# RWKV-7 chain in a hybrid decoder step: two heads per 128 by 128 product, states on diagonal blocks

## The chip, the cores and the metric

The kernel runs on one core of one Trainium2 chip. The metric is the time of one execution on the device in microseconds (us). Three runs of the kernel before took 1861.98, 1864.36 and 1865.9 us; the median, 1864.36 us, is what the change is measured against. One more execution was profiled; its own time stands in the profile section.

## What is computed

One decoder layer for 1024 prompt tokens and 64 sample tokens (8 sequences of 8). A combined projection feeds a sliding-window attention branch and an RWKV-7 branch; both are gated, projected, merged and projected again. The change touches the RWKV-7 branch, 16 heads of 64:

```python
def step(S, inp):
    rt, wt, kt, vt, at, bt = inp
    sa = jnp.einsum('bhvk,bhk->bhv', S, at)
    S = S * wt[:, :, None, :] + sa[..., None] * bt[:, :, None, :] + vt[..., None] * kt[:, :, None, :]
    return S, jnp.einsum('bhvk,bhk->bhv', S, rt)
S_T, ys = lax.scan(step, S0.astype(jnp.float32), xs)
```

The kernel computes it in chunks of 64 tokens: inside a chunk a triangular system is inverted, and between chunks only the 64 by 64 state of each head is handed on.

## The kernel before

**Streams.** `rwkv` (L482) lets six generators share TensorE: `chains`, `merges`, `fronts`, `samples`, `posts` and the dense projections (`stream`). `drive` (L142) writes TensorE's order out by hand while the program is built: it keeps a clock, `self.clk`, to which `mm` (L102, L111) adds the price of each product and `step` 0.06 (WX) for each turn of a stream ahead of the dense one. A stream that yields a number is due that many units after its last turn (or after a named mark); while no stream is due, dense products fill in, four at a time. On the chip TensorE works through this order one by one, and waits wherever an operand isn't there yet. The order of the other engines is made by the compiler's scheduler. Prices before, for n moving columns: n/2400 for the rounded 32-bit type of the dense products (two dense terms per weight half, one record each), n/1200 or n/1700 for a full 32-bit product or a transpose. A full 32-bit product leaves two records in the trace.

**A stage** is 256 prompt tokens (four chunks) of two groups of two heads; there are 16. In each stage:

- `front` (L547) calls `quarter` (L580) for each group. A quarter waits 3.5 units (WD), makes decays and keys, waits 9 units (WB), makes the bonus `bo`, and then the score products `A` of both heads (L713, 64 rows by 128 columns), whose results go to `am` and `ab`; keys and values are transposed (L732, L734) into `kbt` and `vsu`. The first quarter of stage s waits for the mark of chain s-2 (L675).
- `invert` (L740) inverts the 32 by 32 diagonal blocks on VectorE: `ab` goes to DRAM (L726) and comes back in another layout (L753), 31 steps of two instructions each (L760, L762) run, and the result goes to DRAM (L764).
- `merge` (L767) waits 34 units (WI) after the front's mark, loads the inverse into `tr` (L777), transposes parts of it on VectorE (L779), waits 4 units (WM), and makes the off-diagonal blocks with 16 products of 32 by 32 (`q..a`, L790) and 16 more (`q..b`, L795).
- `chain` (L800) goes through four chunks. Each has four heads and, per head, a product with `am` (L826), one with the inverse `tr` (L832), one with `kbt` (L836) and two into the output `y` (L840, L841); between them ScalarE and VectorE copy results out of PSUM (L827, L833) and VectorE updates the state (L850, L851). The waits are 1.7 units before a chunk (WS) and twice 1.0 (WH). At its end it waits for the posts of the stage before (L853).
- `posts` normalise and gate the output; after each fourth stage `sample_chunk` (L863) does the sample tokens of a group.

The PSUM tag "m" has one buffer, shared by fronts, merges, samples and posts; the planner keeps it closed for 1.4 units (HOLD) after each use.

Of the kernel before, what the change touches and what calls it, by code (L numbers as in the profile page):

```python
# [14 lines left out]
P = 128  # L15
# [66 lines left out]
class Prog:  # L82
# [399 lines left out]
    def rwkv(self):  # L482
# [21 lines left out]
        self.qd = QD  # L504
        self.drive([(self.chains(), CHAIN), (self.merges(), CHAIN), (self.fronts(), FRONT), (self.samples(), SAMP),
# [41 lines left out]
    def front(self, s):  # L547

        nc, ep, cp = self.nc, self.ep, self.cp_
        p, q = s // 4, s % 4  # L550
        nm = f"{p}_{q}"
        n2 = 20 if q == 3 else 16
        s1 = self.dp.tile([2, n2, 32, 32], F32, name=f"s1{nm}")
        self.fr[s] = f = dict(s1=s1, s=s, n2=n2, q=[])
        for i in range(2):
            yield from self.quarter(2 * p + i, q, i, f)
        with self.tc.high_priority(offset=INV):
            self.invert(nm, n2, f)
        self.mark(f"f{s}")
# [20 lines left out]
    def quarter(self, g, q, gi, f):  # L580
        nc, ep, cp = self.nc, self.ep, self.cp_
        nm = f"{g}_{q}"
        s1 = f["s1"]
# [23 lines left out]
        zr, zv = E("zr"), E("zv")  # L607
        for z, j in ((zr, 0), (zv, 2)):
            nc.sync.dma_start(z[:, :n], self.d_z[g][j][:, a0:a0 + n])
# [44 lines left out]
        nc.vector.tensor_tensor(KB[:, :4, 0, :], v64(kf), d64(Pi, 1), ALU.mult)  # L654
        nc.vector.tensor_tensor(KB[:, :4, 1, :], v64(aa), d64(Pi, 1), ALU.mult)
        if smp:
            nc.vector.tensor_tensor(o8(RA, 0), s64(zr), d8(Pp, 1), ALU.mult)
            nc.vector.scalar_tensor_tensor(o8(RA, 1), s64(kkn), -1.0, d8(Pp, 0), ALU.mult, ALU.mult)
            nc.vector.tensor_tensor(o8(KB, 0), s64(kf), d8(Pi, 1), ALU.mult)
            nc.vector.tensor_tensor(o8(KB, 1), s64(aa), d8(Pi, 1), ALU.mult)  # L660
# [6 lines left out]
        nc.vector.tensor_tensor(zr[:, :n], ps[:, :n], zv[:, :n], ALU.mult)  # L667
# [5 lines left out]
        if gi == 0:  # L673
            if f["s"] > 1:
                yield f"c{f['s'] - 2}", 0.0  # L675
            f["ab"] = cp.tile([P, f["n2"], HD], F32, tag="ab", name=f"ab{nm}", bufs=2, padded_shape=[P, 20, HD])
            f["vsu"] = cp.tile([P, 4, 2, P], F32, tag="vsu", name=f"vsu{nm}", bufs=2)
            f["pc"] = cp.tile([P, 4, 2, 2], F32, tag="pc", name=f"pc{nm}", bufs=2)
# [4 lines left out]
        S = dict(am=cp.tile([P, 2, 4, P], F32, tag="am", name=f"am{nm}", bufs=4),  # L683
                 tr=cp.tile([P, 8, HD], F32, tag="tr", name=f"tr{nm}", bufs=4),
                 kbt=cp.tile([P, 4, P], F32, tag="kbt", name=f"kbt{nm}", bufs=4),
                 vsu=f["vsu"][:, :, gi, :])
        sets = [(S, 0, 4, 8 * gi)]
        if smp:
            S["smp"] = Z = dict(am=self.pp.tile([P, 2, 1, P], F32, tag="ams", name=f"ams{nm}", bufs=2),
                                tr=self.pp.tile([P, 2, HD], F32, tag="trs", name=f"trs{nm}", bufs=2),  # L690
# [4 lines left out]
            sets.append((Z, 4, 1, 16 + 2 * gi))  # L695
            nc.scalar.activation(Z["pc"], d8(Pp, 8, 1).squeeze(2), AF.Copy)
            nc.scalar.activation(Z["ra"], RA[:, 4, :, :], AF.Copy)
        pend = d64(Pp, 64, 1).squeeze(2)
        nc.scalar.activation(f["pc"][64:128, :, gi, 0], pend[0:64], AF.Copy)
        nc.scalar.activation(f["pc"][64:128, :, gi, 1], pend[64:128], AF.Copy)  # L700
        ident = self.cst(C_ID, P)
        for X, c0, cn, n0 in sets:
            am, tr, kbt, vsu = X["am"], X["tr"], X["kbt"], X["vsu"]
            mi, ms = (C_SI, C_SS) if c0 else (C_MI, C_MS)
            for h in range(2):
                hr = slice(h * 64, h * 64 + 64)
                if c0 == 0:
                    nc.vector.tensor_copy(am[64:128, h, :, 64:128], RA[hr, :4, 1, :])
                    nc.scalar.activation(tr[64:128, 4 * h:4 * h + 4, :], RA[hr, :4, 0, :], AF.Copy)
                yield WA if c0 else 0.0  # L710
                pv = self.ps("a", f"A{nm}{c0}{h}", 2).rearrange("p (c x) -> p c x", c=4)
# [3 lines left out]
                nc.vector.tensor_tensor(am[:, h, :, 0:64], pv[:, :cn, 0:64],  # L715
                                        self.cst(mi, 64).unsqueeze(1).to_broadcast([P, cn, 64]), ALU.mult)
                nc.vector.tensor_tensor(am[0:64, h, :, 64:128], pv[0:64, :cn, 64:128],
                                        self.cst(ms, 64, 0, 64).unsqueeze(1).to_broadcast([64, cn, 64]), ALU.mult)
                abv = ab[64:128, n0 + h * cn:n0 + (h + 1) * cn, :]
                if c0:  # L720
                    nc.vector.tensor_tensor(abv, pv[64:128, 0:1, 64:128], self.cst(ms, 64, 64, 128).unsqueeze(1), ALU.mult)
                else:
                    nc.scalar.activation(abv, pv[64:128, :cn, 64:128], AF.Copy)
            n1 = n0 + 2 * cn
            for i in range(2):
                nc.sync.dma_start(s1[i, n0:n1].rearrange("n j t -> j n t"), ab[64 + 32 * i:96 + 32 * i, n0:n1, 32 * i:32 * i + 32])  # L726
            for b0 in range(0, cn, 2):
                bn = min(2, cn - b0)
                yield None, 0.0, "m"
                ps = self.ps("m", f"t{nm}{c0}{b0}")  # L730
                for c in range(b0, b0 + bn):
                    self.mm(ps[:, (c - b0) * P:(c - b0 + 1) * P], KB[:, c0 + c, :, :].rearrange("p a s -> p (a s)"), ident, transpose=True)  # L732
                for c in range(b0, b0 + bn):
                    self.mm(ps[0:64, 256 + (c - b0) * P:256 + (c - b0 + 1) * P], zv[:, (c0 + c) * 64:(c0 + c + 1) * 64], ident, transpose=True)  # L734
                pv = ps.rearrange("p (c x) -> p c x", c=4)
                nc.scalar.activation(kbt[:, b0:b0 + bn, :], pv[:, :bn, :], AF.Copy)
                nc.scalar.activation(vsu[0:64, b0:b0 + bn, :], pv[0:64, 2:2 + bn, :], AF.Copy)
# [29 lines left out]
    def merge(self, s):  # L767
        nc = self.nc
        nm = f"{s // 4}_{s % 4}"
        yield f"f{s}", WI  # L770
        f = self.fr[s]
        ab, n2 = f["ab"], f["n2"]
        sv = f["s2"][:, :32, :].rearrange("(i n) j t -> i j n t", i=2)
        trs = [f["q"][q]["tr"] for q in range(2)]
        for q, tr in enumerate(trs):
# [4 lines left out]
        for q in range(2 if n2 == 20 else 0):  # L780
            tr = f["q"][q]["smp"]["tr"]
            n0 = 16 + 2 * q
            for i in range(2):
                nc.sync.dma_start(tr[32 * i:32 * i + 32, :, 32 * i:32 * i + 32], sv[i][:, n0:n0 + 2, :])
            nc.gpsimd.memset(tr[32:64, :, 0:32], 0.0)
            nc.gpsimd.memset(tr[0:32, :, 32:64], 0.0)
# [4 lines left out]
        nc.vector.tensor_copy(ab[32:64, 0:16, 0:32], pq[32:64, 0:16])  # L791
        yield None, WH, "m"
        pq = self.ps("m", f"q{nm}b").rearrange("p (n x) -> p n x", x=32)
        for n in range(16):
            self.mm(pq[0:32, n, :], lhsT=ab[32:64, n, 0:32], rhs=trs[n // 8][32:64, n % 8, 32:64], start=True, stop=True)  # L795
        for q, tr in enumerate(trs):
            nc.scalar.activation(tr[0:32, :, 32:64], pq[0:32, 8 * q:8 * q + 8, :], AF.Copy)
        self.mark(f"m{s}")

    def chain(self, s):  # L800
# [8 lines left out]
        if smp:  # L809
            so = self.pp.tile([P, 2, P], F32, tag="so", name=f"so{p}", bufs=1)  # L810
        psy = self.ps("y", f"y{nm}").rearrange("p (i t) -> p i t", i=2)
        heads = [(i, h) for i in range(2) for h in range(2)]
        hs = [slice(h * 64, h * 64 + 64) for h in range(2)]
        up = slice(64, 128)
        for c in range(4):
            first = q == 0 and c == 0
            ps = self.ps("c", f"c{nm}{c}")
            px = ps[0:64, 0:256].rearrange("p (i x) -> p i x", i=2)
            pu = ps[up, 0:256].rearrange("p (i x) -> p i x", i=2)
            pn = ps[up, 256:512].rearrange("p (i x) -> p i x", i=2)  # L820
            lo = slice(0, 64) if first else slice(0, 128)
            xs = cp.tile([P, 2, P], F32, tag="xs", name=f"xs{nm}{c}", bufs=2)
# [660 lines left out]
```

## Time and profile before

| | |
|---|---|
| median of three runs | 1864.36 us |
| profiled execution | 1874.02 us |
| its span, first to last instruction | 1872.2 us |
| TensorE busy over the span | 1783.7 us (95%) |
| VectorE / ScalarE / GpSimd busy | 1123.9 / 963.8 / 359.2 us |
| 80 to 1320 us: RWKV stages with dense work between | 1240 us |
| 1345 to 1872 us: attention, output projections | 527 us |

A row of the trace gives a group of instructions with its engine, line of the kernel, operation, output and inputs by name, and shape (rows by columns of the weights, then the moving operand). TensorE's products are pipelined: a row's duration is that of one record from its issue to its modelled end, and the cost of a record to the stream is the distance to the next one's start.

### The profile page before, as it was taken

What the parts mean: (1) busy time and instruction counts of PE and PEld (TensorE: products, weight loads), DVE (VectorE), ACT (ScalarE), POOL (GpSimd) and SP (SyncE); (2) the same over time, 40 slices, a digit from 0 to 9 for tenths busy, and PEclk for the clock granted to TensorE, in tenths of its full rate; (3) what the DMA queues carried; (4) which work ended last, traced back from release to release, by engine and by line L of the source; (5) the groups of instructions that cost most, each with busy time, mean ns of one, the idle gap of its engine ahead of it and who ended that gap; (6) DMA issues with size and microseconds to landing.
All of it is one profiled execution on the core that took longest, in us unless ns stands there. A gap on an engine that the chain in (4) does not pass through costs nothing.

```text
span 1872.2 us, 35547 instructions
## 1 busy us (share of the span) xinstructions
PE 1783.7 (95%) x13056; PEld 1610.3 (86%) x13056; DVE 1123.9 (60%) x3247; ACT 963.8 (51%) x2442; POOL 359.2 (19%) x356
## 2 busy tenths in 40 slices
PE   5999999999999899999999999999899999999997
PEld 4999988888887788888888888898699899899997
DVE  6325767577567576576676476652566676544443
ACT  5455555554555564655664646632466765432333
POOL 4343222222133112222311121220200000000000
PEclk9999999999999899999999999999899999999999
DMA  4333323332332233333333333322512444374521
GB/s 156 115 114 118 102 82 92 96 100 89 95 110 84 83 89 100 87 108 97 91 91 101 97 100 92 93 80 79 186 49 74 122 126 148 106 222 136 190 98 60
DMA packets 180994, 199.42 MB, mean 107 GB/s; under 512 B 72052, under 2 KB 156388, under 8 KB 180788
## 3 DMA queue, kind: packets, MB, share of 16 engines
q1 hardware_dynamic: 180244, 194.19, 34.5%
q0 software_dynamic: 576, 2.96, 0.5%
q8 instruction: 103, 1.69, 0.4%
q14 instruction: 71, 0.58, 0.1%
HBM read 135.09 MB, written 63.95 MB: 106 GB/s over the span
## 4 chain that ended last, share of the span: by engine, by line
PE 43%; DVE 3%; DMA 2%; issue 1%; ACT 1%; POOL 0%; SPq 0%; DVEq 0%; POOLq 0%; ACTq 0%
PE d L110 24%; PE wo L110 5%; PE y L110 2%; PE c L110 2%; PE s L110 2%; PE o L110 2%; PE pt L108 1%; PE A L110 1%; DMA mb<-d_m 1%; DVE Tt L760 1%; DMA d_w<-mb 1%; DVE klo L1033 0%; PE os L110 0%; PE t L108 0%; PE ss_d L110 0%
## 5 line engine op out<-in xcount | busy, mean ns | idle before, releaser
L110 PE MATMUL d<-hhi,whi 128*128 128x364 f32 (+1 forms) x1656 | 574.6, 347 | 14.8 <-DVE gz L435 7.9
L110 PE MATMUL d<-hlo,whi 128*128 128x364 f32 (+1 forms) x1656 | 553.7, 334 | 7.9 <-DVE hlo L350 7.0
L110 PEld LDWEIGHTS d<-hhi,whi 128*128 128x128 f32 x1656 | 317.9, 192 | 36.9 <-issue 9.3
L110 PE MATMUL d<-hhi,wlo 128*128 128x364 f32 (+1 forms) x1656 | 336.1, 339 | 0.0
L110 PEld LDWEIGHTS d<-hlo,whi 128*128 128x128 f32 x1656 | 318.8, 193 | 12.2 <-DVE hlo L350 9.6
L110 PEld LDWEIGHTS d<-hhi,wlo 128*128 128x128 f32 x1656 | 280.2, 192 | 8.7 <-issue 3.7
L171 POOL TENSOR_TENSOR wlo<-wraw,whi 128x1024 fp32r<-128x1024 f32 x56 | 136.0, 2428 | 353.1 <-PE d L110 128.9
L760 DVE TENSOR_TENSOR Tt<-TM,TR 96x90 f32<-96x90 f32 (+26 forms) x496 | 151.4, 305 | 11.0
L762 DVE TENSOR_TENSOR TR<-TR,Tt 96x90 f32<-96x90 f32 (+26 forms) x496 | 132.1, 266 | 13.7 <-issue 1.2
L170 ACT ACTIVATE whi<-wraw 128x1024 fp32r<-128x1024 f32 x90 | 95.0, 1056 | 77.8 <-PE d L110 69.7
L405 POOL TENSOR_TENSOR zz<-zz,pad 128x364 f32<-128x364 f32 (+1 forms) x75 | 75.8, 1011 | 201.9 <-ACT zz L404 128.4
L833 DVE COPY vsu<-c 64x256 f32<-64x256 f32 x64 | 27.4, 428 | 99.5 <-PE c L110 89.7
L110 PE MATMUL y<-am,vsu 128*64 128x64 f32 x512 | 81.4, 245 | 0.0
L1056 ACT ACTIVATE sc<-sc,st 128x256 f32<-128x256 f32 (+1 forms) x128 | 61.8, 485 | 35.4 <-DVE st L1052 35.1
L110 PE MATMUL y<-tr,xs 64*64 64x64 f32 x480 | 78.0, 243 | 0.0
L403 ACT ACTIVATE pad<-d,prm 128x364 f32<-128x364 f32 (+1 forms) x75 | 40.8, 544 | 61.7 <-PE d L110 51.4
L1317 POOL TENSOR_TENSOR xr<-xr,frs 128x256 f32<-128x256 f32 x2 | 1.8, 932 | 349.1 <-ACT frs L1314 349.1
L110 PE MATMUL d<-yhi,whi 128*128 128x364 f32 (+1 forms) x192 | 65.3, 340 | 0.5 <-DVE mb L1237 0.5
L110 PE MATMUL d<-oh,whi 128*128 128x364 f32 (+1 forms) x192 | 63.5, 331 | 1.3 <-ACT oh L229 1.0
L110 PE MATMUL d<-ylo,whi 128*128 128x364 f32 (+1 forms) x192 | 64.1, 334 | 0.0
L110 PE MATMUL d<-ol,whi 128*128 128x364 f32 (+1 forms) x192 | 63.6, 331 | 0.4 <-DVE ol L230 0.2
L110 PE MATMUL A<-RA,KB 64*128 64x128 f32 x544 | 63.0, 288 | 0.0
(309 smaller groups left out, 3593.4 us busy)
## 6 DMA issues: line engine op xcount, KB each, us to landing
wraw<-in_w SPq DMA_DIRECT2D x93, 512.0 KB
d_z<-zz SPq DMA_DIRECT2D x48, 182.0 KB
d_m<-sp SPq DMA_DIRECT2D x32, 182.0 KB
TM<-s SPq DMA_DIRECT2D x72, 64.0 KB
stageo<-d_o SPq DMA_DIRECT2D x8, 544.0 KB
d_z<-zz SPq DMA_DIRECT2D x24, 180.0 KB
w<-in_lora SPq DMA_DIRECT2D x32, 128.0 KB
bias<-in_biasp SPq DMA_DIRECT2D x16, 256.0 KB
```

The lines of the kernel that those rows point to most:

```text
L108: self.nc.tensor.transpose(out, lhsT, rhs)
L110: self.nc.tensor.matmul(out, lhsT=lhsT, rhs=rhs, **kw)
L170: nc.scalar.activation(hi, raw, AF.Copy)
L171: (nc.vector if self.dve_lo else nc.gpsimd).tensor_tensor(lo, raw, hi.bitcast(F32), ALU.subtract)
L403: nc.scalar.activation(pad[:, 1:1 + m], ps[:, :m], AF.Copy, scale=mu)
L405: nc.gpsimd.tensor_tensor(z[:, :m], z[:, :m], pad[:, 0:m], ALU.add)
L760: nc.vector.tensor_tensor(tv, M[s // 16][:np_, s % 16:s % 16 + 1, s + 1:32].to_broadcast([np_, cc, w]), R[:np_, 0:cc, s:s + 1].to_broadcas ...
L762: nc.vector.tensor_tensor(R[:np_, 0:cc, s + 1:32], R[:np_, 0:cc, s + 1:32], tv, ALU.add)
L833: nc.vector.tensor_copy(vsu[up, c], pu)
L1056: nc.scalar.activation(sc[k], sc[k], AF.Exp, bias=st[:, 0, k:k + 1], accum_out=st[:, 1, k:k + 1])
L1317: en.tensor_tensor(xt[:, dt, :n], xt[:, dt, :n], rst[:, :n], ALU.mult)
```

## The change

Two heads of a group are treated as one operand of 128 rows. The chain's matrices hold one head in rows and columns 0 to 63 and the other in 64 to 127, zero elsewhere; `r0`, `ti` and (for samples) `tss` are fixed tiles whose zeros are written once. The states and values of `vsu` lie on opposite diagonal blocks. Each chain product is then one of 128 by 128 for both heads: per chunk ten products instead of twenty. Copies out of PSUM take one head each and are split between ScalarE and VectorE, a decayed state `sp` is made on GpSimd, and VectorE adds it in with four instructions. `ti` exists once, so `merge` of stage s waits for chain s-1; the output tile `ysb` has one buffer, so a chain waits for the posts of the stage before at its start. Score products of the two heads alternate, as do the 32 by 32 products of `merge`. The planner's prices change. The samples' chunk is treated in the same way.

```diff
-        self.clk += n / 2400 if rhs.dtype == F32R else n / 1200 if lhsT.shape[-1] > 64 else n / 1700
+        self.clk += max(n / 2190, 0.085) if rhs.dtype == F32R else n / 1200 if transpose else max(n / 580, 0.066)
...
         for i in range(2):
             yield from self.quarter(2 * p + i, q, i, f)
+        for h in range(2):
+            for i in range(2):
+                r = 64 * h + 32 * i
+                nc.sync.dma_start(s1[i, h * nh:h * nh + nh].rearrange("n j t -> j n t"), f["ab"][r:r + 32, :nh, 32 * i:32 * i + 32])
...
-        nc.vector.tensor_tensor(KB[:, :4, 0, :], v64(kf), d64(Pi, 1), ALU.mult)
-        nc.vector.tensor_tensor(KB[:, :4, 1, :], v64(aa), d64(Pi, 1), ALU.mult)
...
+        for h, hr in enumerate(halves):
+            for t, j in ((aa, h), (kf, 1 - h)):
+                nc.vector.tensor_tensor(KB[hr, :4, j, :], v64(t)[hr], d64(Pi, 1)[hr], ALU.mult)
...
-                for c in range(cn):
-                    self.mm(pv[:, c, :], lhsT=KB[hr, c0 + c, :, :].rearrange("p a s -> p (a s)"),
-                                     rhs=RA[hr, c0 + c, :, :].rearrange("p a s -> p (a s)"), start=True, stop=True)
...
+            pvs = [self.ps("a", f"A{nm}{c0}{h}", 2).rearrange("p (c x) -> p c x", c=4) for h in range(2)]
+            for c in range(cn):
+                for h, hr in enumerate(halves):
+                    self.mm(pvs[h][:, c, :], lhsT=KB[hr, c0 + c, :, :].rearrange("p a s -> p (a s)"),
+                            rhs=RA[hr, c0 + c, :, :].rearrange("p a s -> p (a s)"), start=True, stop=True)
...
         yield f"f{s}", WI
+        if s:
+            yield f"c{s - 1}", 0.0
...
+        for h in range(2):
+            r = 64 * h
             for i in range(2):
-                nc.sync.dma_start(tr[32 * i:32 * i + 32, :, 32 * i:32 * i + 32], sv[i][:, 8 * q:8 * q + 8, :])
-            nc.gpsimd.memset(tr[32:64, :, 0:32], 0.0)
-            nc.vector.transpose(ab[64:96, 8 * q:8 * q + 8, 0:32], tr[0:32, :, 0:32])
...
+                b = r + 32 * i
+                nc.sync.dma_start(tv[b:b + 32, :, b:b + 32], sv[i][:, h * nh:h * nh + 8, :])
+            nc.vector.transpose(ab[r:r + 32, 0:8, 0:32], tv[r:r + 32, :, r:r + 32])
...
         yield None, WM, "m"
         pq = self.ps("m", f"q{nm}a").rearrange("p (n x) -> p n x", x=32)
-        for n in range(16):
-            self.mm(pq[32:64, n, :], lhsT=ab[64:96, n, 32:64], rhs=ab[64:96, n, 0:32], start=True, stop=True)
...
+        for n in range(8):
+            for r in (0, 64):
+                self.mm(pq[r + 32:r + 64, n, :], lhsT=ab[r:r + 32, n, 32:64], rhs=ab[r:r + 32, n, 0:32], start=True, stop=True)
...
+        if s:
+            yield f"p{s - 1}", 0.0
+        y = self.pp.tile([P, 2, 320], F32, tag="ysb", name=f"ysb{nm}", bufs=1)
...
+            for h in hs:
+                nc.gpsimd.tensor_tensor(sp[h], vsu[h, c, :, h], pc[h, c].unsqueeze(2).to_broadcast([64, 2, HD]), ALU.mult)
             if c:
                 yield WS
-            for i, h in heads:
-                self.mm(px[:, i, hs[h]], lhsT=Q[i]["am"][lo, h, c, 64:128], rhs=vsu[lo, c, i, hs[h]], start=True, stop=True)
-            nc.scalar.activation(xs[0:64], px, AF.Copy)
-            if not first:
-                nc.scalar.activation(xs[up], vsu[up, c], AF.Copy)
+            for i in range(2):
+                self.mm(px[:, i, :], lhsT=Q[i]["am"][:, 1, c].rearrange("p h s -> p (h s)"), rhs=vsu[:, c, i, :], start=True, stop=True)
+            for i in range(2):
+                self.mm(psy[:, c % 2, i, :], lhsT=vsu[:, c, i, :], rhs=Q[i]["r0"][:, :, c, :], start=(c % 2 == 0 and i == 0), stop=False)
+            nc.scalar.activation(xs[hs[0]], px[hs[0], :, hs[0]], AF.Copy)
+            nc.vector.tensor_copy(xs[hs[1]], px[hs[1], :, hs[1]])
             yield WH
-            for i, h in heads:
-                self.mm(pu[:, i, hs[h]], lhsT=Q[i]["tr"][0:64, 4 * h + c, :], rhs=xs[0:64, i, hs[h]], start=True, stop=True)
-            nc.vector.tensor_copy(vsu[up, c], pu)
+            for i in range(2):
+                self.mm(pu[:, i, :], lhsT=Q[i]["ti"][:, c, :], rhs=xs[:, i, :], start=True, stop=True)
+            nc.scalar.activation(vsu[hs[0], c, :, hs[0]], pu[hs[0]], AF.Copy)
+            nc.vector.tensor_copy(vsu[hs[1], c, :, hs[1]], pu[hs[1]])
             yield WH
...
+            for i in range(2):
+                self.mm(pn[:, i, :], lhsT=Q[i]["kbt"][:, c, :], rhs=vsu[:, c, i, :], start=True, stop=True)
+            for i in range(2):
+                self.mm(psy[:, c % 2, i, :], lhsT=vsu[:, c, i, :], rhs=Q[i]["am"][:, 0, c].rearrange("p h s -> p (h s)"), start=False, stop=(c % 2 == 1 and i == 1))
...
+            for i in range(2):
+                for h in hs:
+                    dst = vsu[h, c + 1, i, h] if c < 3 else so[h, i] if smp else self.fr[s + 1]["vsu"][h, 0, i, h]
+                    nc.vector.scalar_tensor_tensor(dst, pn[h, i, h], pc[h, c, i:i + 1], sp[h, i], ALU.mult, ALU.add)
...
-        if s:
-            yield f"p{s - 1}", 0.0
```

## Rows read from the trace of the kernel before

**Rows 1.** Busy time by engine, 80 to 1320 us (length, busy, count, clock).

```profile
80.00:1320.00 1240.00, 1195.13 (x9216) 1060.53 (x9215) 764.97 (x2283) 666.77 (x1725) 302.39 (x293) 0.98 0.33 95
```

**Rows 2.** Timeline of TensorE, one chain chunk: start, us, engine, line, operands.

```profile
938.07 0.32 PE L110 MATMUL d<-hlo,whi 128*128 128x360 f32 x1
938.32 0.68 PE L110 MATMUL c<-vsu,am 128*64 128x64 f32 x8
...
939.20 0.33 PE L110 MATMUL d<-hlo,whi 128*128 128x360 f32 x1
...
942.05 0.65 PE L110 MATMUL d<-hhi,wlo 128*128 128x360 f32 x3
...
945.57 0.33 PE L110 MATMUL d<-hlo,whi 128*128 128x364 f32 x1
```

**Rows 3.** Timeline of TensorE around a 32-bit 128 by 128 product, 1803 us.

```profile
1803.59 0.34 PE L110 MATMUL wo<-mh,whi 128*128 128x416 f32 x1
1803.85 0.94 PE L110 MATMUL fs<-fac,ones 128*128 128x416 f32 x2
...
1804.81 0.35 PE L110 MATMUL wo<-mh,whi 128*128 128x416 f32 x1
```

**Rows 4.** Timeline of TensorE, short products with full-width weights, 1354 us.

```profile
1354.74 0.22 PE L110 MATMUL s<-ks,qs 128*128 128x128 f32 x1
...
1354.91 0.33 PE L110 MATMUL s<-ks,qs 128*128 128x256 f32 x1
```

**Rows 5.** Timeline of TensorE: score, merge and sample products.

```profile
1135.27 1.71 PE L110 MATMUL A<-RA,KB 64*128 64x128 f32 x16
...
1200.96 1.19 PE L110 MATMUL q_2a<-ab 32*32 32x32 f32 x32
...
1001.93 1.11 PE L110 MATMUL ss_a<-ras,sin 64*64 64x16 f32 x32
```

**Rows 6.** Windows of stage 14, last score to merge: dense TensorE records alone.

```profile
1136.90:1201.00 64.10, 39.06 (x204) 1.00 0.32 95
```

**Rows 7.** Timelines: last score products, inverse, last transpose; stages 14, 15, 10.

```profile
1152.46 0.18 DVE L760 TENSOR_TENSOR Tt<-TM,TR 96x31 f32<-96x31 f32 x1
...
1185.88 0.17 DVE L762 TENSOR_TENSOR TR<-TR,Tt 96x11 f32<-96x11 f32 x1
...
1195.85 0.44 DVE L779 STREAM_TRANSPOSE ab<-tr 32x256 f32<-32x256 f32 x1
...
1213.55 0.48 PE L110 MATMUL A<-RA,KB 64*128 64x128 f32 x2
...
1259.15 0.84 DVE L779 STREAM_TRANSPOSE ab<-tr 32x256 f32<-32x256 f32 x2 [3.04 <-DMA tr<-s]
...
852.36 1.16 PE L110 MATMUL A<-RA,KB 64*128 64x128 f32 x11
...
917.62 0.44 DVE L779 STREAM_TRANSPOSE ab<-tr 32x256 f32<-32x256 f32 x1
```

**Rows 8.** Windows of VectorE, the same stretch of stage 14 and its inverse.

```profile
1136.90:1201.00 64.10, 47.93 (x144) 1.00 0.32 95
1152.50:1186.20 33.70, 30.43 (x105) 1.00 0.27 82
```

**Rows 9.** Timeline of TensorE after an idle stretch (brackets: idle before, releaser).

```profile
629.10 0.67 PE L110 MATMUL d<-hhi,whi 128*128 128x364 f32 x1 [6.81 <-DVE gz L435]
...
632.61 0.51 PE L110 MATMUL d<-hlo,whi 128*128 128x364 f32 x1
```

**Rows 10.** Groups by line, 80 to 1320 us: count, busy us, mean ns, idle before.

```profile
L654 DVE TENSOR_TENSOR KB<-e,sg 128x256 f32<-128x256 f32 x32 | 14.8, 462 | 0.1
L721 DVE TENSOR_TENSOR ab<-A,rco 64x64 f32<-64x64 f32 x16 | 3.6, 227 | 0.4
L171 POOL TENSOR_TENSOR wlo<-wraw,whi 128x1024 fp32r<-128x1024 f32 x54 | 131.2, 2429 | 350.5 <-PE d L110 128.9 <-ACT whi L170 110.8 <-DVE TR L762 34.8
L412 POOL TENSOR_TENSOR zz<-zz,pad 128x64 f32<-128x64 f32 x24 | 9.6, 400 | 0.1
```

More of the change, by code (lines that the diff above doesn't have):

```diff
@@ L504, in rwkv @@
         self.qd = QD
+        cp = self.cp_
+        self.ti = cp.tile([P, 2, 4, P], F32, name="ti")
+        self.tss = cp.tile([P, 2, P], F32, name="tis")
+        self.r0s = [cp.tile([P, 2, 4, HD], F32, name=f"r0{x}") for x in range(4)]
+        for t in (self.ti, self.tss, *self.r0s):
+            nc.gpsimd.memset(t, 0.0)
         self.drive([(self.chains(), CHAIN), (self.merges(), CHAIN), (self.fronts(), FRONT), (self.samples(), SAMP),
@@ L582, in quarter @@
         nm = f"{g}_{q}"
-        s1 = f["s1"]
         smp = q == 3
@@ L606, in quarter @@
         w2, zk, kkn, parts = self.ahead.pop((g, q))
-        zr, zv = E("zr"), E("zv")
-        for z, j in ((zr, 0), (zv, 2)):
-            nc.sync.dma_start(z[:, :n], self.d_z[g][j][:, a0:a0 + n])
+        zr, zv = E("zr"), ep.tile([P, 5, 2, HD], F32, tag="zv", name=f"zv_{nm}", bufs=1)
+        nc.sync.dma_start(zr[:, :n], self.d_z[g][0][:, a0:a0 + n])
+        for j in range(2):
+            nc.sync.dma_start(zv[:, :n // 64, j, :], self.d_z[g][2][:, a0:a0 + n].rearrange("p (c s) -> p c s", s=64))
         yield f"pf{g}_{q}", WD, "m"
@@ L722, in quarter @@
                 else:
[L723 to L737, printed above, removed]
+                    nc.scalar.activation(abv, pv[hr, :cn, 64:128], AF.Copy)
@@ new lines, in quarter @@
+            yield None, 0.0, "m"
+            ps = self.ps("m", f"t{nm}{c0}k").rearrange("p (c x) -> p c x", c=4)
+            for c in range(cn):
+                self.mm(ps[:, c, :], KB[:, c0 + c, :, :].rearrange("p a s -> p (a s)"), ident, transpose=True)
+            nc.scalar.activation(kbt, ps[:, :cn, :], AF.Copy)
+            yield None, 0.0, "m"
+            ps = self.ps("m", f"t{nm}{c0}v").rearrange("p (c x) -> p c x", c=4)
+            for c in range(cn):
+                self.mm(ps[:, c, :], zv[:, c0 + c].rearrange("p a s -> p (a s)"), ident, transpose=True)
@@ L738, in quarter @@
+            for h, hr in enumerate(halves):
+                vr = halves[1 - h]
+                nc.scalar.activation(vsu[vr, :, hr], ps[vr, :cn, hr], AF.Copy)
         f["q"].append(S)
@@ L792, in merge @@
+        for r in (0, 64):
+            nc.vector.tensor_copy(ab[r + 32:r + 64, 0:8, 0:32], pq[r + 32:r + 64, 0:8])
         yield None, WH, "m"
         pq = self.ps("m", f"q{nm}b").rearrange("p (n x) -> p n x", x=32)
[L794 to L797, printed above, removed]
+        for n in range(8):
+            for r in (0, 64):
+                self.mm(pq[r:r + 32, n, :], lhsT=ab[r + 32:r + 64, n, 0:32], rhs=tv[r + 32:r + 64, n, r + 32:r + 64], start=True, stop=True)
@@ L809, in chain @@
         if smp:
-            so = self.pp.tile([P, 2, P], F32, tag="so", name=f"so{p}", bufs=1)
-        psy = self.ps("y", f"y{nm}").rearrange("p (i t) -> p i t", i=2)
-        heads = [(i, h) for i in range(2) for h in range(2)]
+            so = self.pp.tile([P, 2, HD], F32, tag="so", name=f"so{p}", bufs=1)
+        if s:
+            yield f"p{s - 1}", 0.0
+        y = self.pp.tile([P, 2, 320], F32, tag="ysb", name=f"ysb{nm}", bufs=1)
         hs = [slice(h * 64, h * 64 + 64) for h in range(2)]
-        up = slice(64, 128)
@@ L815, in chain @@
         for c in range(4):
-            first = q == 0 and c == 0
             ps = self.ps("c", f"c{nm}{c}")
[L818 to L822, printed above, removed]
+            px = ps[:, 0:256].rearrange("p (i x) -> p i x", i=2)
@@ L861, in chain @@
+            if c % 2:
+                for h in hs:
+                    nc.scalar.activation(y[h, :, c * 64 - 64:c * 64 + 64].rearrange("p i (c t) -> p i c t", c=2),
+                                         psy[h, :, :, h].rearrange("p c i t -> p i c t"), AF.Copy)
+        self.ysb[s] = [y[:, i] for i in range(2)]
+        if smp:
+            for i in range(2):
+                nc.sync.dma_start(self.O["pwkv"][2 * p + i], so[:, i, :])
         self.mark(f"c{s}")
@@ L864, in sample_chunk @@
         nc, cp = self.nc, self.cp_
-        am, tr, kbt, vsu = Z["am"], Z["tr"], Z["kbt"], Z["vsu"]
+        am, kbt, vsu = Z["am"], Z["kbt"], Z["vsu"]
         sin = self.sin
+        halves = [slice(h * 64, h * 64 + 64) for h in range(2)]
         yield f"sin{g}", 7.0, "m"
@@ L869, in sample_chunk @@
         for b in range(NB):
-            for h in range(2):
-                hr = slice(h * 64, h * 64 + 64)
+            for hr in halves:
                 self.mm(ps[hr, :, b * 8:b * 8 + 8], lhsT=sin[hr, b, :], rhs=Z["ra"][hr, :, b * 8:b * 8 + 8], start=True, stop=True)
-        sx = self.pp.tile([P, 2, HD], F32, tag="sx", name=f"sx{g}", bufs=1)
-        nc.scalar.activation(sx, ps, AF.Copy)
+        sx = self.pp.tile([P, 3, HD], F32, tag="sx", name=f"sx{g}", bufs=1)
+        nc.scalar.activation(sx[:, 0:2], ps, AF.Copy)
@@ L875, in sample_chunk @@
+        nc.vector.tensor_copy(sx[:, 2], ps[:, 1])
         yield None, WH, "m"
         ps = self.ps("m", f"ss{g}_b")
-        for h in range(2):
-            hs = slice(h * 64, h * 64 + 64)
-            self.mm(ps[0:64, hs], lhsT=sx[:, 1, :], rhs=self.cst(C_ID, P)[:, hs], start=True, stop=False)
-            self.mm(ps[0:64, hs], lhsT=am[0:64, h, 0, 64:128], rhs=vsu[0:64, 0, hs], start=False, stop=True)
-        xs = self.pp.tile([P, P], F32, tag="ve", name=f"xss{g}", bufs=1, padded_shape=[P, NB * HD])
@@ L882, in sample_chunk @@
-        nc.scalar.activation(xs[0:64], ps[0:64, 0:128], AF.Copy)
+        self.mm(ps[:, 0:P], lhsT=sx[:, 1:3, :].rearrange("p a s -> p (a s)"), rhs=self.cst(C_ID, P), start=True, stop=False)
+        self.mm(ps[:, 0:P], lhsT=am[:, 1, 0].rearrange("p h s -> p (h s)"), rhs=vsu[:, 0, :], start=False, stop=True)
+        xs = self.pp.tile([P, HD], F32, tag="ve", name=f"xss{g}", bufs=1, padded_shape=[P, NB * HD])
+        for hr in halves:
+            nc.scalar.activation(xs[hr], ps[hr, hr], AF.Copy)
```

132 lines of the change are left out of this document (59 added, 73 removed).

## The prediction

> **What bounds the kernel now.** I read the windows first: from 80 to 1320 us, where the change lies, TensorE is busy for 1195.1 of 1240 us and VectorE for 765.0 [rows 1]. So TensorE's work sets the time of this stretch, and only 1240 - 1195.1 = 44.9 us of it are idle. Next I read the timeline of one chunk for what the chain's products cost, and then the way from a stage's last score product over the inverse on VectorE to the merge, because TensorE's order is written out by a planner and TensorE stands still wherever an operand is late. The reader should see two budgets: TensorE microseconds saved, and the time that the order leaves for the inverse.
>
> **Part 1: the chain's products.** In the chunk shown, the `am` group costs the distance from the dense record before it to the second after it, 939.20 - 938.07 = 1.13 us, less two dense records at 0.165, so 0.80 us [rows 2]. I take the same for the group with the inverse, which has the same count. `kbt` and both products of `y` together: 945.57 - 942.05 = 3.52, less four dense records, 2.86 us [rows 2]. Sum 4.46 us a chunk, times 64 chunks: 285 us. This includes what the change of tile shape costs in the dense records beside a group.
>
> After it, eight of the ten products have 128 moving columns and 128 by 128 weights. The nearest row is the 32-bit sum over 416 columns: from 1803.59 to 1804.81 are 1.22 us for two such records and two dense ones of 0.187, so 0.85 us for two [rows 3]. The score products put one record of 128 columns at 1.64/16 = 0.103 us with 64 rows of weights [rows 5]; 128/416 of the sum's bare 0.347 is 0.107. I take 0.107, and 0.155 a group for entering and leaving (0.85 - 2 x 0.347). The two products with `ti` have 64 columns under full weights: two records with full weights start 0.17 us before the third [rows 4], so 0.085 each; bounds are half the 0.107 and the whole. Chunk: 16 x 0.107 + 4 x 0.085 + 3 x 0.155 = 2.52 us, times 64 = 161 us. **Gain 124 us**; with no entry cost and 0.053 for the short ones, 162; with the 0.33 a group that the old shape pays (0.80 less 8 x 0.058), and 0.107 throughout, 84.
>
> A rule of the Trainium skill speaks against full weights here: TensorE: Matmul & The Clock Gate, section "LDWEIGHTS (loading the stationary operand)", says that a load's time goes by its columns, at 1.2 a nanosecond, 107 ns for 128. The pair just read took 85 ns each, so the trace differs and decides; by the rule the gain would be 6 us less (64 x 4 x 0.022).
>
> **Part 2: alternating products.** 272 score products are 32 groups of about 1.64 us [rows 5]. If heads on different rows of the array ran side by side, half would go. The sample products, which alternate in rows and columns, put 32 records into 1.11 us [rows 5], 0.035 each, while eight of the chain's 64-column ones follow at 0.058; that is overlap, though of another shape. I take 20 of the possible 27 us; floor 0. The merge's 32 groups of 1.19 us [rows 5]: 10 of possible 16. The samples' fewer products and the wider value transposes: 4 us together, 2 to 6. **Sum of TensorE work: -158 us**, bounds -86 and -211.
>
> By the Trainium skill, TensorEngine Tiling (Array Packing), "Key Properties", tiles work independently; the sample rows agree, and by it alone the score products would give the whole 27 us.
>
> **Part 3: the planner's clock, and where the stalls go.** Between the last score product of stage 14 and its merge the plan has 34 + 4 units, 1.4 of hold and the transposes: about 42. In that stretch, 204 dense records of 360 to 364 columns count 30.8 units by the old price [rows 6]; the rest is cheaply priced chain and front work. On the chip it took 64.1 us, 1.5 us a unit. The new price calls a dense record 0.166, which is what it takes, and a full product of 128 columns 0.22 for two records of 0.107. So 42 units become about 45 us (three for group entries that are not priced). The inverse doesn't get shorter. From the end of the scores to the end of the last transpose: stage 14, 1136.9 to 1196.3, 59.4 us; stage 15, 1214.0 to 1260.0, 46; stage 10, 853.4 to 918.1, 64.6 [rows 7]. I read all 16 in this way; they lie between these last two, with the middle at 58 to 59. Of stage 14's, 15.6 us pass before the first instruction of the inverse (two trips through DRAM), 33.6 in it, and 10 in the trips after it [rows 7].
>
> VectorE can't make up for it: it did 47.9 us of work in the 64.1 us, and 30.4 in the 33.7 of the inverse [rows 8]. The new window is shorter than its work in the old one. The change adds to it: two more key products a quarter, 32 x 2 x 0.46 = 29 us [rows 10], and a chunk's nine small instructions near 0.23 [rows 10] instead of three larger ones, about even. So at the merge TensorE waits 59 - 45 = 14 us in a typical stage: 16 x 14 = **+224 us**. Bounds: the shortest stage gives 1 us a stage, 16; a stage like the tenth, 20 each, 320. Below nothing is excluded for a wait. After an idle stretch of 6.8 us eleven dense records took 632.61 - 629.10 = 3.5 us, 0.32 each instead of 0.165, half the clock, 1.2 instead of 2.4 GHz: 1.7 us lost [rows 9], 16 times: **+26** (0 to 26). Most of today's 44.9 us of idle time falls into these windows and is covered by the longer wait: **-30** (0 to -40).
>
> **Part 4: the rest.** Merge s now waits for chain s-1 and its load into `ti` stands on SyncE's queue with stores and weight loads behind it; in the plan the chain before ends ahead of the 34 units, so I put it at nothing; without that cover, a load and a transpose late, 3 to 5 us a stage, part of the bounds above. The chain's new wait for the posts holds only the chain's turn; dense work stands behind it in TensorE's order and runs. The split copies: half-width, on two engines, nothing on the path. GpSimd gets 128 products of 64 by 128, about 0.4 each as the 128 by 64 ones take [rows 10]: 51 us beside 302 of 1240 [rows 1], off the path unless it queues behind a weight product of 2.4 us [rows 10]. The strided value load: one more issue a quarter, off the path. Attention's order is drawn by the same clock, with dense prices up by a tenth; I put it at nothing, at worst a few us, since the rows here don't show it.
>
> **Sum:** -158 + 224 + 26 - 30 = +62 us. The profiled execution's 1874.0 would become 1936; the median lies 9.7 below it, so **1926 us**.
>
> **The rivals.** *The inverse fits the shorter window* (faster). Price: if TensorE's standing still lets VectorE give the inverse its whole time, so that a merge waits 5 us as in a stage slightly above the shortest, 16 x 5 = 80 replace 224, and 10 of the clock's 26 remain: -158 + 80 + 10 - 30 = -98, 1766 us. It decides from a wait of about 10 us a stage: 16 x 10 = 160 balances part 2's sum. For it: a waiting TensorE sends no new work to VectorE, and stage 15 has done it in 46 us. Against it: 90% of VectorE's time in the inverse is taken today. *GpSimd enters the chain's loop* (slower still). Each state update needs `sp`; if every third of the 64 x 2 waits for one weight product, 43 x 2.4 = 103 us come on top, half of them hidden by the chunk's waits: 1977 us. Against it: `sp` can start 4 to 5 us before it is needed. *Gain and stalls cancel*: waits of 9 to 10 us, 1864 us.
>
> **How the numbers follow.** The stalls at the merge as sized 0.50 (own range 1880 to 1990), the inverse fits 0.37 (1700 to 1855), GpSimd 0.08, cancelled 0.05. So slower 0.58, same 0.05, faster 0.37, with 0.2%, some 4 us, as what a measurement of this kernel can tell from no change. The range takes in most of the fast case and the bounds of the slow one: 1755 to 1995, which leaves out about 0.1 on each side.
>
> **What would show it.** In the changed profile the waits of TensorE should name the merge's products (`q..a`), released by the transposes at the line that now is `merge`'s, in sum 150 us or more, and TensorE's clock should dip behind each. The chain's records should be 1280, in groups with about 0.107 us a record, and a chunk's own cost near 2.5 us. The scores should take half their time. VectorE should pass 800 us in the RWKV stretch. The prediction is wrong if TensorE's idle time there stays below 100 us, if the way from scores to transposes falls under 50 us, or if a full-width record costs more than 0.13 us.

## The result, and the profile after

The changed kernel takes **2001.3 us** (median), against 1865.1 for the kernel before in the same series: ratio 1.073, 95% interval 1.070 to 1.076. The sign of the forecast was right; the time lies above its 1926 us and just above its range. The mechanism on record is not the one that made it slower.

TensorE's row of the page of after, and its clock, in 40 slices of the span:

```profile
PE   6998889898988989999899765455689999999998
...
PEclk8999898899999999999999855555689999999999
```

Windows of after, for the stretch that [rows 1] show for before (length, then TensorE, weight loads, VectorE, ScalarE, GpSimd busy, clock, DMA share, GB/s). The last chain product runs at 1452 us here, at 1312 before:

```profile
80.00:1128.00 1048.00, 955.35 (x6871) 910.26 (x6869) 667.39 (x2030) 564.96 (x1449) 304.75 (x341) 0.96 0.35 103
1128.00:1452.00 324.00, 181.75 (x1020) 144.46 (x1020) 174.56 (x566) 90.90 (x259) 41.67 (x74) 0.54 0.15 41
```

The hole in slices 23 to 29 is the result. From 1127.7 to 1453.1 us there is no dense product at all: the stock of dense work is used up, and only the RWKV branch is left, which keeps TensorE busy for 182 of 324 us, at a clock of 0.54, near the lower of its two levels (1.2 of 2.4 GHz). Before, dense products ran through to the last chain; the longest gap between two of them up to there was 7.1 us.

From 80 us to the first attention product, TensorE's idle time and its work (distances from one record's start to the next one's, idle time taken off) are:

| | before | after | difference |
|---|---|---|---|
| first attention product at | 1354.7 | 1488.7 | +134.0 |
| TensorE idle | 53.8 | 244.8 | +191.0 |
| TensorE's work | 1220.8 | 1163.9 | -56.9 |
| of it chain | 241.3 | 196.3 | -45.0 |

Why the dense work ran out stands in the order of the products from one chain to the next. TensorE's timeline of after: the end of chain 4, with score and merge products that answer [rows 5], its posts (`gc`, `gv`, once for each group), and the start of chain 5:

```profile
596.74 0.61 PE L110 MATMUL c<-vsu,kbt 128*128 128x128 f32 x4
597.18 0.61 PE L110 MATMUL y<-am,vsu 128*128 128x128 f32 x4
597.72 1.16 PE L110 MATMUL A<-RA,KB 64*128 64x128 f32 x16
598.81 0.65 PE L108 MATMUL t_20k<-con,KB 128*128 128x128 f32 x4
...
603.39 0.69 PE L110 MATMUL q_1a<-ab 32*32 32x32 f32 x32 [0.18 <-ACT vsu L756]
606.19 0.69 PE L110 MATMUL q_1b<-ti,ab 32*32 32x32 f32 x32
...
611.61 0.28 PE L110 MATMUL gc<-shic,cen 128*128 128x256 f32 x1
...
617.16 0.28 PE L110 MATMUL gv<-shiv,bone 128*128 128x256 f32 x1
...
630.04 0.28 PE L110 MATMUL gc<-shic,cen 128*128 128x256 f32 x1
...
635.68 0.28 PE L110 MATMUL gv<-slov,bone 128*128 128x256 f32 x1
635.79 0.61 PE L110 MATMUL c<-vsu,am 128*128 128x128 f32 x4
```

Merge 5 is done at 606.9, yet chain 5 starts at 635.8, in the very next record after its predecessor's posts. That holds for all 15 hand-overs: 0.1 to 0.4 us lie between the posts' last product and the chain's first. So chain and posts run one after the other:

| read from the timelines, us | before | after |
|---|---|---|
| length of a chain, mean | 36.8 | 31.3 |
| end of a chain to its own posts' last product, mean of the first 15 | 59.5 | 48.6 |
| end of a chain to the next one's start, mean | 33.2 | 48.8 |
| start of the merge's last group to the chain's start, sum of 16 | 44 | 566 |
| stage period, from chain start to chain start, mean | 69.9 | 80.4 |

The chain itself became shorter. The column of before also shows that the loop could be read from the trace of before: 36.8 + 59.5 is more than 69.9, so posts overlapped the next chain in each stage but the last two.

The waits of TensorE in the stretch without dense work (sum, times, longest):

```profile
PE bo L110 <- ACT shib L235: 22.7, 4, 10.9
PE q_3a L110 <- DVE ab L801: 17.2, 2, 15.7
PE q_1a L110 <- DVE ab L801: 16.4, 2, 15.6
PE c L110 <- DVE vsu L861: 15.6, 20, 0.9
PE q_2a L110 <- DVE ab L801: 8.2, 2, 7.4
```

The forecast's waits, `q..a` released by the transposes, are there for 42 us in all, but nearly all in this tail, where nothing fills them; ahead of 1128 us they come to under 1 us. Groups of after by line, which answer [rows 10] (count, busy us, mean ns, idle before):

```profile
L872 DVE SCALAR_TENSOR_TENSOR vsu<-c,pc,sp 64x64 f32<-64x64 f32 x240 | 67.9, 283 | 39.3 <-PE c L110 34.9
...
L673 DVE TENSOR_TENSOR KB<-e,sg 64x256 f32<-64x256 f32 x128 | 64.9, 524 | 1.7 <-ACT sg L648 0.9
...
L848 POOL TENSOR_TENSOR sp<-vsu,pc 64x128 f32<-64x128 f32 x128 | 52.9, 414 | 243.1 <-DVE vsu L872 236.7 <-ACT pc L713 1.4
...
L856 DVE COPY xs<-c 64x128 f32<-64x128 f32 x64 | 18.8, 294 | 50.5 <-ACT xs L855 49.5
L861 DVE COPY vsu<-c 64x128 f32<-64x128 f32 x64 | 18.8, 294 | 42.8 <-ACT vsu L860 41.6
```

The last two rows are a second find: VectorE's half of each split copy waits for ScalarE's half. In 64 of 64 pairs of either kind it starts 32 ns or more after the other has ended. The halves do not run side by side.

### The profile page after: what moved, and what is told of

It reads as the page before. It is cut to its first block, busy times and chain, and to the rows that moved or that the text cites. A ratio compares the mean times of both kernels' runs of the same rounds, so it can differ in the third digit from the quotient of the medians.

```text
span 2001.6 us, 33550 instructions
## 1 busy us (share of the span) xinstructions
PE 1722.8 (86%) x11744; PEld 1605.5 (80%) x11744; DVE 1204.1 (60%) x3563; ACT 955.5 (48%) x2430; POOL 405.9 (20%) x490
## 5 line engine op out<-in xcount | busy, mean ns | idle before, releaser
L781 DVE TENSOR_TENSOR TR<-TR,Tt 96x90 f32<-96x90 f32 (+26 forms) x496 | 137.6, 277 | 14.2
L779 DVE TENSOR_TENSOR Tt<-TM,TR 96x90 f32<-96x90 f32 (+26 forms) x496 | 136.8, 276 | 14.4 <-DVE pad L402 0.3
L848 POOL TENSOR_TENSOR sp<-vsu,pc 64x128 f32<-64x128 f32 x128 | 52.9, 414 | 243.1 <-DVE vsu L872 236.7
L872 DVE SCALAR_TENSOR_TENSOR vsu<-c,pc,sp 64x64 f32<-64x64 f32 x240 | 67.9, 283 | 39.3 <-PE c L110 34.9
L110 PE MATMUL c<-vsu,kbt 128*128 128x128 f32 x256 | 56.2, 356 | 30.7 <-DVE vsu L861 30.6
L650 DVE TENSOR_SCALAR kkn<-kn 128x256 f32<-128x256 f32 (+1 forms) x32 | 14.1, 441 | 109.6 <-PE kn L110 109.4
L110 PEld LDWEIGHTS c<-vsu,kbt 128*128 128x128 f32 x256 | 45.9, 246 | 40.0 <-DVE vsu L861 39.7
L940 POOL TENSOR_TENSOR ysb<-ysb,gn 128x256 f32<-128x256 f32 (+1 forms) x32 | 26.2, 820 | 233.0 <-ACT gn L939 185.6
L673 DVE TENSOR_TENSOR KB<-e,sg 64x256 f32<-64x256 f32 x128 | 64.9, 524 | 1.7 <-ACT sg L648 0.9
```

Source lines behind the costliest of these rows:

```text
L673: nc.vector.tensor_tensor(KB[hr, :4, j, :], v64(t)[hr], d64(Pi, 1)[hr], ALU.mult)
L779: nc.vector.tensor_tensor(tv, M[s // 16][:np_, s % 16:s % 16 + 1, s + 1:32].to_broadcast([np_, cc, w]), R[:np_, 0:cc, s:s + 1].to_broadcas ...
L781: nc.vector.tensor_tensor(R[:np_, 0:cc, s + 1:32], R[:np_, 0:cc, s + 1:32], tv, ALU.add)
L848: nc.gpsimd.tensor_tensor(sp[h], vsu[h, c, :, h], pc[h, c].unsqueeze(2).to_broadcast([64, 2, HD]), ALU.mult)
L872: nc.vector.scalar_tensor_tensor(dst, pn[h, i, h], pc[h, c, i:i + 1], sp[h, i], ALU.mult, ALU.add)
L940: nc.gpsimd.tensor_tensor(y, y, rs, ALU.mult)
```

## The experiments

Ratios are against the kernel before, run on the same chip in the same series.

**First, the two suspects apart.** Theory 1: the chain's early wait puts the posts into the chain's loop. Theory 2, as recorded: the new prices shorten the windows.

e1, the wait moved behind the products of the second chunk (and the output tile with it):

```diff
-        if s:
-            yield f"p{s - 1}", 0.0
-        y = self.pp.tile(...)
...
+            if c == 1:
+                if s:
+                    yield f"p{s - 1}", 0.0
+                y = self.pp.tile(...)
```

> The changed kernel with one edit: the chain's turn waits for the posts of the stage before not ahead of its first chunk but after the products of its second, where the output tile is first written. Theory 1 (posts in the loop: in the changed kernel chain s starts only when the posts of s-1 are done, and these start only when chain s-1 is done, so a stage takes a chain of 28 us plus posts of 38 us and more, and the dense work runs out at 1128 us): two of four chunks, some 13 us a stage, leave the loop; the stage period falls from about 72-84 to about 60-70 us and the time to 1830-1900 us. Theory 2 (as recorded: the new prices make the planned windows too short and TensorE waits for the inverse at the merge): the edit leaves the windows as they are, 1990-2010 us.

1977.7 us, ratio 1.058 (1.054 to 1.061). Both missed. The wait now lies inside the chain, which grows from 31.3 to 59.9 us; the period falls only to 78.0. Two chunks are left in the loop, but from the start of the third to the chain's end they take 23.2 us in the mean, in after 13.0. A wait of TensorE that after has for 1.1 us explains most of it; below it stands ScalarE's copy that ends it in stage 1:

```profile
PE y L110 <- ACT ysb L876: 102.5, 15, 10.6
```

```profile
310.04 0.77 ACT L876 ACTIVATE ysb<-y 64x256 f32<-64x256 f32 x2 [3.53 <-DMA d_y<-ysb]
```

The planner's mark for the posts stands at their last product (297.6 us there). The one output tile comes free only after the posts' last steps on other engines and its store (11 of the 15 first copies name the store, four name nothing), and until then the third chunk's `y` products stand still. So e1 exchanges one wait for another and doesn't settle the theories.

e2, the prices of before in the changed kernel:

```diff
-        self.clk += max(n / 2190, 0.085) if ...
+        self.clk += n / 2400 if ...
```

> The changed kernel with the old prices of the planner's clock. Theory 2: the windows are long again on the chip (about 1.4 us a unit), waits at the merge vanish, 1840-1920 us. Theory 1: the loop of chain and posts has the same units and each unit takes more time on the chip, the dense work runs out as early or earlier, 1980-2060 us.

2012.9 us, 1.077 (1.075 to 1.080), period 80.7: as theory 1 has it, and 12 us above after. In the changed kernel the prices explain none of the loss.

e3, the new prices alone in the kernel before (the same line, the other way round):

> The kernel before with the new prices alone. Theory 2: the window of 42 units from the scores to the merge becomes about 46 us where the way over the inverse takes 46 to 65, TensorE waits some 14 us in each of 16 merges, 1950-2090 us. Theory 1: without the early wait nothing holds the chain back; the plan only gets tighter, 1850-1900 us.

1997.7 us, 1.069 (1.064 to 1.073): as theory 2 has it in size, but not in place. Its window up to the last chain (columns as above), and its largest waits of TensorE:

```profile
80.00:1407.00 1327.00, 1209.19 (x8851) 1061.95 (x8850) 745.55 (x2268) 652.73 (x1690) 302.31 (x291) 0.91 0.29 84
```

```profile
PE bo L110 <- ACT shib L235: 16.8, 6, 4.3
PE q_0a L110 <- DVE ab L779: 11.1, 3, 9.7
PE y L110 <- ACT ysb L857: 10.1, 2, 5.3
```

All `q..a` waits for transposes come to 27.5 us, not some 200. The way from last score to merge shrank from 63.9 to 59.0 us in the mean (16 stages each), not to 45. To the first attention product the 134 us are 64 us of idle time in many small waits and 70 us by which the same work was slower, at a clock of 0.91 against 0.98 [rows 1].

e5, the chain's wait for the posts ahead of its first chunk, in the kernel before:

> The kernel before with one edit: the chain's wait for the posts of the stage before stands ahead of its first chunk instead of after its last. Theory 1: chain (about 38 us) and posts (about 38 us) now follow one another, the stage period grows from 70 to 80 us or more, dense work runs out, 1950-2060 us. Theory 2: the wait holds only the chain's turn and dense work goes on behind it, 1860-1875 us.

2049.1 us, 1.096 (1.093 to 1.100); period 82.5, no dense work from 1180 to 1495 us. One moved wait makes the signature of after.

**Second, causes together.** e4 is e1 with the prices of before:

> The changed kernel with both suspected causes taken back in part: prices of before, and the chain's wait for the posts moved from its start to just ahead of its first copy into the output tile (second chunk). If the two causes together are the loss (each keeps the other's from showing): the posts have two chunks less in the loop, the windows have their old 64 us, so the stage period falls from about 80 to 65-70 us, no stretch without dense records over 60 us, 1800 to 1880 us. If a third cause in the chain (GpSimd's product, the split copies, the merge's wait for the chain before) holds it: 1940 us or more, with the stretch still there.

1968.7 us, 1.055 (1.052 to 1.058), a gap of 192 us without dense work: missed. It has the same wait as e1 for the one output tile, 93.5 us in 13 stages (chain 53.8, period 76.9), so it says little about the two causes.

e7 takes posts out of the loop: two output tiles, prices as changed. Room comes from single buffers for `xs` and `sp`, and from tiles shared with others.

```diff
-        if s:
-            yield f"p{s - 1}", 0.0
-        y = ..., tag="ysb", name=f"ysb{nm}", bufs=1)
+        if s > 1:
+            yield f"p{s - 2}", 0.0
+        y = ..., tag="ysb", name=f"ysb{nm}", bufs=2)
```

> The changed kernel with two output tiles alone, prices as changed. If the new prices cost by themselves what they cost the kernel before (about 133 us) and the posts were the rest: 1830 to 1930 us, TensorE's waits at the merges and the inverse back, no stretch without dense records. If the early wait was all that matters in the changed kernel: as the one with the old prices, under 1810 us. If neither: near 2000 us.

1868.6 us, 1.002 (1.0005 to 1.004): **133 us of the loss are this one wait**. What the single buffers cost by themselves wasn't tried. Period 69.0, chain's wait after the merge 129 us in sum instead of 566, longest gap between dense products 13 us. The posts two stages back still hold chains 4, 8 and 12, which start in the record behind them: some 98 of the 129 us.

e6 is e7 with the prices of before:

> The changed kernel with prices of before and two output tiles, so that a chain waits at its start for the posts two stages back (room made by single buffers for the chain's copy and decayed state, and by shared tiles in the sample chunk). If posts in the loop plus short windows are the whole loss: the TensorE work saved shows, 1864 - 158 plus up to 100 of stalls left, 1710 to 1810 us, no stretch without dense records before the last chain ends. If the merge's wait for the chain before or the chain's own new operations also bind: above 1864 us.

1847.3 us, 0.990 (0.987 to 0.993): 1% faster than before, but 37 us above the expected range. The new prices cost 21 us here.

e8, the merge's wait for chain s-1, alone in the kernel before (`yield f"c{s - 1}", 0.0` after the front's mark):

> The kernel before with one line added: merge of stage s waits, ahead of its loads, for the mark of chain s-1, as the change has it. The recorded forecast puts it at nothing: within 0.5% of 1864 us. If the wait binds (chain before ends later than the window of 34 units): each microsecond of delay in 16 stages shows, 1880 us or more.

1865.0 us, 0.999 (0.998 to 1.001): nothing there, as forecast.

**Third, what e6 still loses.** Its idle time was 154 us to the first attention product, before 53.8. The largest waits of TensorE in e6, and one copy in its timeline:

```profile
PE c L110 <- DVE xs L854: 25.8, 18, 3.1
PE c L110 <- DVE vsu L859: 20.6, 21, 3.8
```

```profile
682.11 0.25 ACT L858 ACTIVATE vsu<-c 64x128 f32<-64x128 f32 x1
682.27 0.25 DVE L781 TENSOR_TENSOR TR<-TR,Tt 120x91 f32<-120x91 f32 x1
...
682.56 0.29 DVE L859 COPY vsu<-c 64x128 f32<-64x128 f32 x1
...
682.91 0.71 PE L110 MATMUL c<-vsu,kbt 128*128 128x128 f32 x4 [0.50 <-DVE vsu L859]
```

ScalarE's half ends at 682.36, VectorE's starts at 682.56, TensorE waits 0.50 us. In the median VectorE starts 0.57 (`xs`) and 0.32 us (`vsu`) after ScalarE's end: it has the inverse, as here, and key products in its queue. The trace of before lists no wait of a chain product for such a copy.

e9, e6 with both halves on ScalarE:

```diff
-            nc.vector.tensor_copy(xs[hs[1]], px[hs[1], :, hs[1]])
+            nc.scalar.activation(xs[hs[1]], px[hs[1], :, hs[1]], AF.Copy)
...
-            nc.vector.tensor_copy(vsu[hs[1], c, :, hs[1]], pu[hs[1]])
+            nc.scalar.activation(vsu[hs[1], c, :, hs[1]], pu[hs[1]], AF.Copy)
```

> Base: the changed kernel with two output tiles and old prices (1847.3 us). Edit: the second half of each of the chain's two copies out of PSUM goes from VectorE to ScalarE. In the base VectorE's half never starts before ScalarE's has ended, and TensorE waits 46 us for it (25.8 and 20.6). If VectorE's queue behind the inverse is what makes it late: these 46 us fall below 15, and the time to 1800-1825 us. If the wait comes from two halves one after the other, on whichever engine, or ScalarE's queue takes its place: the waits stay at 30 us or more under ScalarE's name, 1835-1860 us.

1811.3 us, **0.969 (0.967 to 0.972)**. TensorE's largest waits in it:

```profile
PE bo L110 <- DVE ysb L931: 19.7, 4, 8.8
PE c L110 <- DVE vsu L870: 13.0, 13, 3.0
...
PE c L110 <- ACT vsu L859: 4.3, 8, 0.8
...
PE c L110 <- ACT xs L854: 1.4, 2, 0.8
```

The 46 us became 5.7, while the chain's wait for the state update (L870) rose from 2.2 to 13.0. To the first attention product idle time fell by 17 us, and the same products took 15 us less. Two copies in a row on ScalarE take 0.56 us from the first's start to the second's end; split, with nothing between them, 0.27 + 0.03 + 0.29 = 0.59. So what cost was mainly VectorE's queue between them.

e10 and e11, longer waits in the plan (WH 1.0 to 1.5, WB 9 to 11) on e6 and on e9:

> Same base. Edit: two of the planner's waits longer, 1.0 to 1.5 units after a product that is copied out, 9 to 11 units before the bonus. If TensorE's idle time in the base (141 us up to the last chain, before: 45) is the planner's waits being too short for copies that now come one after the other, dense work takes their place: idle time under 100 us, 1810-1835 us. If it is VectorE's lateness whatever the plan: within 0.5% of 1847 us.

> Both edits on the same base. If the copies' place and the waits' length are two costs of their own: the lower of the two and 10 to 20 us less, 1790-1820 us. If they are one cost: as the better of the two, within 0.4%.

1890.8 us (1.012, 1.010 to 1.015) and 1865.6 us (0.999, 0.997 to 1.000), both missed: 43 and 54 us slower than their bases. The period of e10 rose from 69.4 to 71.7 us and dense work was missing from 1225 to 1326 us. Two waits grew at once, so which of them lengthened the stage isn't told.

e12, the copies on ScalarE in the changed kernel as it was:

> The changed kernel (early wait, new prices, one output tile) with one edit: the second half of each of the chain's two copies goes from VectorE to ScalarE. If the loop of chain and posts sets the stage's period, a shorter chain shows in the period only as far as the chain is in it: four chunks, some 46 us in all 16 stages, 1955 to 1985 us, and the stretch without dense records stays above 200 us. If the serial copies were the main loss even here: 1920 us or less. If TensorE's standing idle covers them: within 0.3% of 2001 us.

1989.3 us, 1.064 (1.062 to 1.067): 12 us, less than expected. With posts in the loop, shorter copies hardly show.

e14, e9 with the new prices:

> Same base, with the new prices. If the new prices cost what they cost with the split copies (1868.6 - 1847.3 = 21 us): 1826-1838 us. If the prices matter only together with late copies: within 0.3% of 1811 us. If as in the kernel before (133 us): 1900 us or more.

1854.7 us, 0.993 (0.990 to 0.995): 43 us, more than expected. Its `q..a` waits for transposes are 16.7 us.

e13, e9 with half of the key products on GpSimd:

```diff
-                nc.vector.tensor_tensor(KB[hr, :4, j, :], ...)
+                (nc.gpsimd if t is aa else nc.vector).tensor_tensor(KB[hr, :4, j, :], ...)
```

> Base: two output tiles, old prices, copies on ScalarE (1811.3 us, TensorE idle for 125 us up to the last chain). Edit: half of the key products, 64 of 128 by 0.42 us, 27 us, go from VectorE to GpSimd. If VectorE's added work is what TensorE still waits for in the fronts (the bonus): idle time falls by 10 to 30 us, 1785-1803 us. If GpSimd's slower products only make the keys later: 1811-1835 us.

1804.5 us, 0.966 (0.963 to 0.968). This is the lowest time, but its interval and e9's overlap; idle time fell by 5 us only. On GpSimd such a product takes 0.83 us in the mean, so this is no test of VectorE's load as a whole.

## Why the prediction was right or wrong

**Parts 1 and 2, TensorE's work (-158): right, a little too large.** It can be read in e9, where dense work doesn't run out:

| 80 us to attention, us | before | e9 | difference | forecast |
|---|---|---|---|---|
| chain | 241.3 | 141.6 | -99.7 | -124 |
| scores | 59.7 | 43.1 | -16.6 | -20 |
| merge products | 36.7 | 20.0 | -16.7 | -10 |
| samples, transposes, others | 123.1 | 115.9 | -7.2 | -4 |
| dense | 760.1 | 759.0 | -1.1 | in chain |
| sum | 1220.8 | 1079.6 | -141.2 | -158 |

A chunk's records cost 3.77 us before and 2.21 in e9. The forecast's 4.46 counted the shape change in the neighbouring dense records too; that share didn't come back, and dense work takes as long as before. The median distance of a full-width record is 0.112 us (forecast 0.107). Of the short products with `ti` it is 0.111, not the 0.085 that I had taken from [rows 4]. The two records there belong to different products (`ks`, then `klo`), each of a single record, and were no measure for this one. The Trainium skill (TensorE: Matmul & The Clock Gate, "LDWEIGHTS (loading the stationary operand)") gives a load P / 1.2 ns for P columns, 107 ns for 128: here the measured 111 lies near it, and setting it aside was wrong, by 64 x 4 x 0.026 = 7 us. The 0.155 a group for entering didn't show: twenty records at 0.111 are already the 2.21 us. It rested on 0.347 us a record, which stands in no row; it is the old price, 416/1200.

In after itself only 57 of the 141 us show: its tail runs near half clock, and its chain products cost 196.3 us in all, 141.6 in e9.

**Part 3, stalls at the merge (+224, +26, -30): wrong.** The premise, that 42 units become 45 us, fell in e3: the way was 59.0 us. In the mean 6.8 us of it are idle, and its clock is 0.92 (before: 2.9 us and 0.98). By estimate, with 52 us of work at 0.92 instead of 0.98, these two make up 10 of the 14 us that 45 lacks; the rest is open. The stalls at the merge were 27.5 us there, and 16.7 in e14. As a loss of the changed kernel the term is wrong altogether (e2). What the new prices cost depends on what else binds: 131 us in the kernel before, 21 beside the split copies, 43 without them, -12 under the loop. Why these differ is left open.

**Part 4, the failed step.** "The chain's new wait for the posts holds only the chain's turn; dense work stands behind it in TensorE's order and runs." Dense work did run, for 1048 us, and then there was none. The step asked what stands behind the wait on the engine, and not what the waited-for work itself waits for: posts start at the chain's end, so the wait closes a loop chain, posts, chain of 31.3 + 48.8 = 80.1 us, longer than the 69.9 us in which dense work had filled a stage. It costs 133 us (after against e7), 183 in the kernel before (e5).

**Part 4, the split copies: wrong** ("half-width, on two engines, nothing on the path"). They cost 36 us once the loop is open (e6 to e9), 12 in the changed kernel as it was (e12). The Trainium skill (PSUM — Partial Sum Buffer, "PSUM bank collisions raise a hardware error") says that two engines must not touch the same bank and 32 partitions at a time, while different partition groups of one bank may be read at once. The halves here lie on different partitions and still ran one after the other, 64 of 64 times; whether the shared bank or the shared output tile orders them wasn't tried.

**Part 4, the rest: right as far as it was tried.** The merge's wait costs nothing in the kernel before (e8). In after it binds: up to merge 12 each merge is done 8 to 10 us after the chain before it, and then the chain waits for the posts anyway; what the merge's wait costs without that wasn't tried. GpSimd's products take 0.41 us and hold up nothing that shows: of VectorE's 39.3 us of idle time before the state update, 34.9 end with TensorE's product. Attention takes 512.9 us after its first product, 517.5 before.

**The rivals.** None gave its time. The condition of the first held: the waits at the merge are 42 us in sum, well under its 160, but the loop took the gain. GpSimd's named the right kind of place, a loop that lengthens the chain, with another engine. In "What would show it", waits at `q..a` far under 150 us say that the step is wrong, whatever the sign. Its three conditions for "wrong" all stayed silent: 244.8 us idle, 59 us in the mean from scores to transposes, 0.112 us a record. That the time came out slower, and near the upper bound, is luck.

**Still open:** e9 has 83 us more idle time than before (136.7 against 53.8), in small waits on VectorE and ScalarE at the bonus, the samples and the state update. The posts two stages back still hold six of its chains (4, 5, 8, 9, 12, 13). VectorE is busy for 797 of 1173 us there, 765 of 1240 before [rows 1]; e13 doesn't settle whether that is the reason.

## What to carry to other kernels

When a change adds a wait to a serial chain, write down what the awaited work waits for. If it is the chain, add up one round and compare it with the stage's period: both stood in the trace of before, 36.8 + 59.5 us against 69.9. That sum was too long, the round came to 80.1, but it gave the sign. Independent work behind a wait hides it only while there is some left, so look where it ends. Splitting a copy between two engines gains only if the halves overlap; here they didn't, and the busier engine's queue came onto the path.

## What the hardware showed beyond that

- Score products of two heads on different rows of the array overlap in part: 16 records took 1.09 us (597.72 to 598.81) instead of 1.64 [rows 5], not the half. Alternating 32 by 32 products went from 1.19 [rows 5] to 0.69 us for 32.
- A 128 by 128 product of 64 moving columns costs as much as one of 128: 0.111 and 0.112 us.
- With only the RWKV branch to do, TensorE was busy for 56% of the time and had a clock of 0.54; while it had dense work, 0.96.
